# Two transformer blocks in split fp32 products: head, tables, expert hand-over and two stage entries rearranged

## The chip, the cores and the metric

The kernel runs on one core of one Trainium2 chip. The metric is the device time of one execution in microseconds (us), the median of several runs. The core has a matrix engine (TensorE, PE in the profile), two elementwise engines (VectorE, DVE; ScalarE, ACT), GpSimd (POOL), and SyncE (SP), which here only requests transfers. PEclk is the share of TensorE's full clock that was granted.

## The reference

256 tokens of width 1024 go through two blocks, all in fp32. Cut to its core:

```python
def first_block(x, ...):
    x = x + short_conv_mixer(rmsnorm(x, norm_mix[0]), w_in, w_conv, w_out)   # c_gate * u, 3-tap conv, b_gate
    x = x + swiglu(rmsnorm(x, norm_ffn[0]), w_gate, w_up, w_down)            # width 2816
    x = x + mla_mixer(rmsnorm(x, norm_mix[1]), ...)                          # 8 heads, latent q and kv
    return x + moe_swiglu(rmsnorm(x, norm_ffn[1]), router, ...)              # 8 experts of 2048, top 2

def second_block(x, ...):
    proj = rmsnorm(x, attn_norm_g) @ w_in                 # qa, ka, va, qb, kb, vb
    out_a = gqa_axial_attention(rope(norm(qa)), rope(norm(ka)), va)
    out_b = rmsnorm(differential_attention(norm(qb), norm(kb), vb, lam, rel_bias), b_subln_g)
    x = x + concatenate([out_a, out_b]) @ w_out
    return x + square(relu(rmsnorm(x, mlp_norm_g) @ w_up)) @ w_down          # width 4096
```

## The kernel before

Every product is made of three. A weight is split in two parts: `w_hi` is a rounding copy made by ScalarE (L115), `w_lo` what is left, made by VectorE (L116), and the activations are split likewise; hi times hi, lo times hi and hi times lo are added in PSUM (`mm3`, L231). PSUM has 8 banks of 128x512.

Weights come in loads of 1 MB, requested by SyncE (`load`, L96) into a ring of seven slots (`raws`); while the experts run, three more slots (`raws2`, L845) belong to the ring. A load is split into two units of 128x1024 (`split`, L107), for which a ring of five pairs exists (`units`). `weight_parts` (L159) is a generator that gives the units in the order in which the stages use them. `get` (L210) takes the next and keeps one more made; `prepare(n)` (L216) makes n of them at once, so that their splits stand earlier on ScalarE and VectorE. Each engine does its instructions in program order as the scheduler leaves it. `behind(...)` (L85) orders what is issued inside it after the given instructions, and `fence` holds instructions which the next split must follow.

The stages: the head (`first_norm`, L358) squares x, scales it by the rms factor and the gain, transposes it into `hT` (features on partitions) and splits it. The short convolution has twelve loads of `w_in`, each for two products of `proj_T` (L236), in the order c, u, b. At the end of each stage an `Entry` (L400) adds the sums to x, multiplies by the next gain (`xg`), transposes and splits, one half of the tokens (t) at a time; the rms factor follows later. The second half's entry (`finish`) stands inside the next stage's first products. Inside the dense layer small tables (rope frequencies, gains, bias rows, lambda vectors, router weights) are requested behind the second gated pair (L644 to L647), by ScalarE's queue.

The experts run one after the other over at most 128 gathered tokens. `gather` (L1017) picks the tokens of two experts by products with a one-hot `pick`; `wide` (L1040) makes gate and up, `turned_features` transposes, the down product collects in `yb`. `gated_y` (L1049) multiplies by the gate and splits into `y`; `scatter` (L1057) puts the rows of one expert back by products with the one-hot `put`, and adds to x.

In the second block `columns_in` (L1160) makes 256 columns of the joint input projection for both halves; the first are the keys (`keys_a`), whose result is rotated and normed into `yd` and transposed (L1205), then the queries (`yq`). The MLP's first two products are made for one half of the tokens, then for the other.

## Time and profile before

| what | us |
|---|---|
| median of 3 runs (1299.24 to 1303.44) | 1300.73 |
| the profiled execution's own time | 1304.09 |
| its span | 1302.3 |
| TensorE busy in it | 1267.9 |
| VectorE, ScalarE busy | 994.9, 801.7 |

The rows further below come from this one execution. A timeline row has the start, the duration, the engine, the line in the kernel, the operation, `out<-in`, the shape and a count where like instructions follow one another; in brackets stands how long the engine was idle before it and what ended that. "Q" behind an engine's name is its queue of requests.

### The profile page before, as it was taken

What the parts mean: (1) busy time and instruction counts of PE and PEld (TensorE: products, weight loads), DVE (VectorE), ACT (ScalarE), POOL (GpSimd) and SP (SyncE); (2) the same over time, 40 slices, a digit from 0 to 9 for tenths busy, and PEclk for the clock granted to TensorE, in tenths of its full rate; (3) what the DMA queues carried; (4) which work ended last, traced back from release to release, by engine and by line L of the source; (5) the groups of instructions that cost most, each with busy time, mean ns of one, the idle gap of its engine ahead of it and who ended that gap; (6) DMA issues with size and microseconds to landing.
All of it is one profiled execution on the core that took longest, in us unless ns stands there. A gap on an engine that the chain in (4) does not pass through costs nothing.

```text
span 1302.3 us, 17506 instructions
## 1 busy us (share of the span) xinstructions
PE 1267.9 (97%) x6551; PEld 1065.9 (82%) x6551; DVE 994.9 (76%) x1283; ACT 801.7 (62%) x1089; POOL 76.3 (6%) x96
## 2 busy tenths in 40 slices
PE   8999999999998999999999999999998999999998
PEld 7998788888777888888888887878787887888887
DVE  6665655556867999999988989898898697765654
ACT  5444445445665877778867776777766566544442
POOL 0000100000502000000000000000000432000000
PEclk9999999999998999999999999999998999999999
DMA  9854655744434999989999999989987533456620
GB/s 318 280 168 175 217 192 129 245 142 149 163 127 174 372 379 353 374 306 360 356 335 320 326 359 337 349 324 361 349 307 243 177 106 114 144 188 196 192 97 33
DMA packets 156799, 320.26 MB, mean 246 GB/s; under 512 B 7788, under 2 KB 50823, under 8 KB 156712
## 3 DMA queue, kind: packets, MB, share of 16 engines
q1 hardware_dynamic: 151104, 313.54, 68.5%
q10 hardware_dynamic: 5608, 5.58, 1.8%
q8 instruction: 52, 0.85, 0.3%
q14 instruction: 35, 0.29, 0.1%
HBM read 317.00 MB, written 2.10 MB: 245 GB/s over the span
## 4 chain that ended last, share of the span: by engine, by line
PE 62%; DVE 2%; ACT 1%; POOL 1%; DMA 1%; issue 1%; POOLq 0%; ACTq 0%
PE bank L58 38%; PE yb L58 13%; PE acc L58 8%; PE bank L1076 1%; DVE w_lo L116 1%; PE po L58 1%; ACT w_hi L115 1%; DMA bias<-wide_d 1%; POOL yq L1198 0%; DMA raw<-in_moe_w_up_dram 0%; PE bank L1279 0%; POOL s L1301 0%; ACT s L1295 0%; POOL raq L1185 0%; PE bank L392 0%
## 5 line engine op out<-in xcount | busy, mean ns | idle before, releaser
L116 DVE TENSOR_TENSOR w_lo<-raw,w_hi 128x1024 fp32r<-128x1024 f32 (+2 forms) x600 | 709.6, 1218 | 189.6 <-ACT w_hi L115 177.4
L115 ACT CAST w_hi<-raw 128x1024 fp32r<-128x1024 f32 (+2 forms) x600 | 605.3, 1043 | 270.6 <-PE bank L58 149.1
L58 PE MATMUL bank<-w_hi,xT 128*128 128x512 f32 x1024 | 318.9, 393 | 0.9 <-ACT w_hi L115 0.9
L58 PEld LDWEIGHTS bank<-w_hi,xT 128*128 128x128 f32 x1024 | 190.4, 188 | 39.4 <-ACT w_hi L115 1.7
L58 PE MATMUL bank<-w_lo,xT 128*128 128x512 f32 x512 | 201.6, 394 | 1.1 <-DVE w_lo L116 1.1
L58 PE MATMUL bank<-w_hi,hT 128*128 128x256 f32 (+1 forms) x672 | 162.9, 338 | 2.4 <-ACT w_hi L115 2.0
L58 PEld LDWEIGHTS bank<-w_hi,hT 128*128 128x128 f32 x672 | 116.2, 192 | 15.8 <-ACT w_hi L115 2.3
L58 PE MATMUL bank<-hT,w_hi 128*128 128x256 f32 (+1 forms) x656 | 116.2, 326 | 2.2 <-DVE hT L394 1.4
L58 PEld LDWEIGHTS bank<-w_lo,xT 128*128 128x128 f32 x512 | 96.1, 188 | 26.2 <-DVE w_lo L116 6.4
L58 PE MATMUL bank<-w_lo,hT 128*128 128x256 f32 (+1 forms) x336 | 110.8, 337 | 0.0
L58 PEld LDWEIGHTS bank<-hT,w_hi 128*128 128x128 f32 x656 | 96.8, 194 | 11.1 <-DVE hT L394 1.7
L58 PE MATMUL yb<-w_hi,a_hi 128*128 128x512 f32 x256 | 101.3, 396 | 0.0
L58 PE MATMUL yb<-w_hi,a_lo 128*128 128x512 f32 x256 | 101.3, 396 | 0.0
L58 PE MATMUL yb<-w_lo,a_hi 128*128 128x512 f32 x256 | 95.6, 399 | 0.0
L58 PE MATMUL acc<-w_hi,a_hi 128*128 128x512 f32 x216 | 84.9, 393 | 0.0
L58 PE MATMUL acc<-w_lo,a_hi 128*128 128x512 f32 x216 | 84.4, 391 | 0.0
L58 PE MATMUL acc<-w_hi,a_lo 128*128 128x512 f32 x216 | 84.3, 390 | 0.0
L58 PEld LDWEIGHTS bank<-w_lo,hT 128*128 128x128 f32 x336 | 64.6, 192 | 6.9 <-DVE w_lo L116 0.5
L58 PE MATMUL bank<-hT,w_lo 128*128 128x256 f32 (+1 forms) x464 | 65.2, 284 | 0.0
L58 PEld LDWEIGHTS bank<-hT,w_lo 128*128 128x128 f32 x464 | 62.2, 194 | 2.3
L58 PEld LDWEIGHTS yb<-w_hi,a_lo 128*128 128x128 f32 x256 | 48.2, 188 | 11.3
L58 PEld LDWEIGHTS yb<-w_hi,a_hi 128*128 128x128 f32 x256 | 48.2, 188 | 11.4
(318 smaller groups left out, 1373.3 us busy)
## 6 DMA issues: line engine op xcount, KB each, us to landing
raw<-in_moe_w_gate_dram SPq DMA_DIRECT2D x64, 1024.0 KB, 6.5
raw<-in_moe_w_up_dram SPq DMA_DIRECT2D x64, 1024.0 KB, 6.6
raw<-in_moe_w_down_dram SPq DMA_DIRECT2D x64, 1024.0 KB, 6.4
raw<-in_w_up_dram SPq DMA_DIRECT2D x16, 1024.0 KB, 5.4
raw<-in_w_down_dram SPq DMA_DIRECT2D x16, 1024.0 KB, 4.9
raw<-in_conv_w_in_dram SPq DMA_DIRECT2D x12, 1024.0 KB, 12.1
raw<-in_ffn_w_gate_dram SPq DMA_DIRECT2D x11, 1024.0 KB, 5.1
raw<-in_ffn_w_up_dram SPq DMA_DIRECT2D x11, 1024.0 KB, 12.5
```

Source lines behind the costliest of these rows:

```text
L58: return nc.tensor.matmul(o, lhsT, rhs, start=start, stop=stop)
L115: halves[:] = [nc.scalar.copy(hv, v), nc.vector.tensor_tensor(lv, v, hv.bitcast(F32), op=OP.subtract)]
L116: nc.vector.tensor_tensor(lv, v, hv.bitcast(F32), op=OP.subtract)]
L1076: nc.tensor.transpose(bt[:, fs], sg[:, fs], ident)
```

## The change

**Head.** x is loaded in quarters and transposed as it is; the gain is multiplied behind the transposes, the rms factor only on the results (`inv_row`, a row made by one product of ones and a diagonal). The first 256 columns of `w_in` come in two loads of half size, and the first product runs in halves of the features. **Tables.** 21 requests go from ScalarE's queue to SyncE's. **Experts.** Copies of the gather all go to ScalarE; two experts' rows are put back in one sum; two units are prepared ahead of `gated_y`; the odd experts' `y` takes a slot of the three more. **Entries.** Ahead of the second block's attention and of its MLP, three and two units are prepared before the first products, and 512 columns of the first half of the tokens stand ahead of the second half's entry.

```diff
@@ -101,7 +102,7 @@
-        nc.sync.dma_start(v, src.rearrange("(a p) b -> p a b", p=P))
+        loads[:] = [nc.sync.dma_start(v, src.rearrange("(a p) b -> p a b", p=P))]
@@ -159,9 +160,14 @@
-        upper = [columns_of(w[:, g * D : (g + 1) * D]) for g in (1, 2, 0)]
-        for _ in range(0, KD, 2):
-            for u in upper:
+        for rs in blocks(2, 512):
+            v = load(w[rs, D : D + 256], 4, 256)
+            for fs in blocks(2):
+                yield split(v[:, :, fs])
+        upper = [columns_of(w[:, g * D : (g + 1) * D], 256 * (g == 1)) for g in (1, 2, 0)]
+        for f0 in range(0, KD, 2):
+            for u in upper[f0 == 0 :]:
                 yield next(u)
                 yield next(u)
@@ -213,6 +219,11 @@
+    def take(n):
+        prepare(n)
+        return [ready.pop(0) for _ in range(n)]
@@ -233,19 +244,30 @@
+    def first_proj_T(h):
+        banks = [bank()[:, :T] for _ in range(2)]
+        for n in range(2):
+            for o in banks:
+                hi, lo = get()
+                for w, s in ((hi, 0), (hi, 1), (lo, 0)):
+                    for k in range(4):
+                        mm(o, w[:, k], h[s][:, 4 * n + k], n == 0 and k == 0 and w is hi and s == 0,
+                           n == 1 and k == 3 and w is lo)
+        return banks
@@ -355,35 +377,67 @@
-    def first_norm(g):
+    def first_entry(g):
...
+        xg = acts.tile([P, 2, D], F32, tag="xn", name="xgT", bufs=1).rearrange("p a (b k t) -> p (a b) k t", b=2, k=4)
+        his, xgs, los = [], [], []
+        def multiplied(j):
+            t, n = quarters[j]
+            v = bank().rearrange("p (k t) -> p k t", k=4)
+            for k in range(4):
+                turned = nc.tensor.transpose(v[:, k], x[:, t, (4 * n + k) * P : (4 * n + k + 1) * P], ident)
+            xgs.append(nc.vector.tensor_tensor(xg[:, j], v, g[:, 4 * n : 4 * n + 4, None].to_broadcast([P, 4, P]),
+                                               op=OP.mult))
+            return turned
...
+        def rounded(j):
+            his.append(nc.scalar.copy(place(hi, j), xg[:, j]))
+        def left(j):
+            los.append(nc.vector.tensor_tensor(place(lo, j), xg[:, j], place(hi, j).bitcast(F32), op=OP.subtract))
...
+        for j in range(4):
+            with behind(*los[-1:], *xgs[-1:]):
+                turned = multiplied(j)
+            if j < 3:
+                with behind(*his[-1:]):
+                    rounded(j)
+            if j == 1:
+                with behind(xgs[1]):
+                    left(0)
+        with behind(xgs[3]):
+            left(1)
+        fence[:] = [his[2], los[1]]
+        prepare(2)
+        with behind(halves[0]):
+            rounded(3)
+        for j in (2, 3):
+            with behind(halves[1], los[-1]):
+                left(j)
+        fence[:] = [his[3], los[3]]
+        return (hi, lo), turned
...
+    def first_factors(pool):
+        ss, ms, inv, rs = (pool.tile([P, 2], F32, name=n, bufs=1) for n in ("ss0", "ms0", "inv0", "rs0"))
+        junk = acts.tile([P, D], BF16, tag="sg", name="junk")
+        with behind(*halves):
+            for t in range(2):
+                nc.scalar.activation(junk, x[:, t], AF.Square, accum_out=ss[:, t : t + 1])
+        nc.vector.tensor_scalar(ms, ss, 1.0 / D, EPS, op0=OP.mult, op1=OP.add)
+        nc.vector.reciprocal(inv, ms)
+        nc.gpsimd.tensor_tensor(rs, ms, mhalf[:, :2], op=OP.pow)
+        diag = pool.tile([P, 2, P], F32, name="diag", bufs=1)
...
+            nc.vector.tensor_scalar(diag[:, t], ident, inv[:, t : t + 1], None, op0=OP.mult)
+        return rs, diag
@@ -419,11 +475,17 @@
-            left = []
+            left, last = [], []
             for n, ns in enumerate(blocks(2, 512)):
-                if acc is not None:
+                stack = ExitStack()
+                stack.enter_context(behind(*last))
+                if acc is not None and self.factor is not None:
+                    nc.vector.scalar_tensor_tensor(x[:, t, ns], acc[n], self.factor[:, t : t + 1], x[:, t, ns],
+                                                   op0=OP.mult, op1=OP.add)
+                elif acc is not None:
                     nc.vector.tensor_tensor(x[:, t, ns], x[:, t, ns], acc[n], op=OP.add)
-                nc.vector.tensor_tensor(self.xg[:, t, ns], x[:, t, ns], g[:, ns], op=OP.mult)
+                stack.close()
+                last = [nc.vector.tensor_tensor(self.xg[:, t, ns], x[:, t, ns], g[:, ns], op=OP.mult)]
@@ -515,9 +577,9 @@
         rb = pool.tile([32, 4], F32, name="rb")
-        nc.scalar.dma_start(rb, i["rel_bias_2"])
+        nc.sync.dma_start(rb, i["rel_bias_2"])
         onehot = pool.tile([32, 512], F32, name="onehot")
-        nc.scalar.dma_start(onehot, i["c_bucket"])
+        nc.sync.dma_start(onehot, i["c_bucket"])
@@ -543,32 +605,43 @@
-        for b, ns in zip(g, blocks(2, 512)):
-            mm(b, one, row[:, ns], True, True)
-        turn_rows(rows, 0, 24)
+        ones = cp.tile([P, P], F32, name="ones_f", bufs=1)
+        nc.vector.memset(ones, 1.0)
+        turn_rows(g_rows, 32, KD)
+        h, turned = first_entry(cols[:, 32 : 32 + KD])
+        with behind(turned, fence[1]):
+            turn_rows(rows, 0, 24)
...
-            pc = proj_T(h, f0 == 0)
             c_sb = cp.tile([P, 2, T], F32, name="c_sb")
-            copied = nc.scalar.copy(c_sb, pc)
-            pu = proj_T(h)
+            if f0 == 0:
+                pc = first_proj_T(h)
+                first_rs, diag = first_factors(cp)
+                pu = proj_T(h)
+                b = bank()[:, :T]
+                with behind(products[-1]):
+                    mm(b, ones, diag.rearrange("p t k -> p (t k)"), True, True)
+                nc.scalar.copy(inv_row, b)
+                for f in range(2):
+                    nc.vector.tensor_tensor(c_sb[:, f], pc[f], inv_row, op=OP.mult)
+            else:
+                pc = proj_T(h)
+                nc.vector.tensor_tensor(c_sb, pc, inv_row[:, None, :].to_broadcast([P, 2, T]), op=OP.mult)
+                pu = proj_T(h)
...
-                with behind(copied):
+                with behind(done):
@@ -583,9 +656,10 @@
-        entry = Entry()
+        entry = Entry(first_rs)
@@ -629,7 +703,7 @@
                 prod = nc.vector.scalar_tensor_tensor(sg[t], pu[t], rs[:, t : t + 1], sg[t], op0=OP.mult, op1=OP.mult)
-            with behind(silu, prod):
+            with behind(silu, prod, *loads):
                 for table in tables if made[0] in (0, 2) else ():
                     next(table, None)
@@ -1015,18 +1089,18 @@
-            for src, dst, copy in ((h_hi, x_hi, nc.scalar.copy), (h_lo, x_lo, nc.vector.tensor_copy)):
+            for src, dst in ((h_hi, x_hi), (h_lo, x_lo)):
...
-                    copy(dst[:, k0 : k0 + 2], v)
+                    nc.scalar.copy(dst[:, k0 : k0 + 2], v)
...
-            put = ep.tile([P, T], F32R, name="put", bufs=2)
+            put = ep.tile([P, T], F32R, name="put", bufs=3)
@@ -1046,29 +1120,27 @@
-        def gated_y(place, yb, last):
-            y = room_y.tile([P, 2, D], F32R, tag="raw", name="y") if last else \
-                acts.tile([P, 2, D], F32R, tag="xn", name="y", bufs=1)
+        def gated_y(place, yb, odd):
+            y = (room_y if odd else acts).tile([P, 2, D], F32R, tag="raw" if odd else "xn", name="y",
+                                               **({} if odd else {"bufs": 1}))
...
-        def scatter(put, y, done=None):
...
+        def rows_back(rows, halves):
+            banks = [[bank() for _ in range(2)] for _ in halves]
+            for last, (put, y) in enumerate(rows):
+                for t, pair in zip(halves, banks):
+                    for s in range(2):
+                        for b, ns in zip(pair, blocks(2, 512)):
+                            mm(b, put[:, blocks(2)[t]], y[:, s, ns], last + s == 0, last + s == 2)
+            return banks
+        def scatter(rows):
+            for t in range(2):
+                for b, ns in zip(rows_back(rows, (t,))[0], blocks(2, 512)):
+                    nc.vector.tensor_tensor(x[:, t, ns], x[:, t, ns], b, op=OP.add)
@@ -1106,10 +1179,9 @@
-                if g == E * NC:
-                    prepare(3)
                 if c0 == NC - 1:
-                    done = gated_y(place, yb, g == E * NC)
+                    prepare(3 if g == E * NC else 2)
+                    rows.append(gated_y(place, yb, len(rows) == 1))
@@ -1122,12 +1194,8 @@
         entry = Entry()
-        def enter(t):
-            entry.half(t)
-            prepare(4)
-        scatter(*done, enter)
+        for t, banks in enumerate(rows_back(rows, (0, 1))):
+            entry.half(t, banks)
@@ -1157,13 +1225,33 @@
+        def first_columns_in():
+            os = [bank().rearrange("p (t c) -> p t c", t=2) for _ in range(2)]
+            ws = take(3)
+            part_in(os[0], ws, 0, range(KD))
+            ws = [ws[:2], ws[2:] + take(1)]
+            part_in(os[1], ws[1], 0, range(4))
+            rest_of_entry()
+            part_in(os[1], ws[1], 0, range(4, KD))
+            for o, w in zip(os, ws):
+                part_in(o, w, 1, range(KD))
+            return os
...
+            if first:
+                return first.pop(0)
...
-                if t and not bias:
-                    rest_of_entry()
@@ -1357,6 +1445,7 @@
+        first = first_columns_in()
@@ -1380,11 +1469,11 @@
-                ws = [get(), get()] if first and f0 == 0 else None
+                ws = take(2) if first and f0 == 0 else None
                 for ts in blocks(2) if ws else (slice(0, T),):
-                    if ts.start:
-                        entry.finish()
                     for f, o in enumerate(banks):
+                        if ws and f and ts.start == 0:
+                            entry.finish()
                         hi, lo = ws[f] if ws else get()
                         for k in range(KD):
```

TensorE at the program's start, before (`row` is the gain, `rows` the taps, `xn` the normed x):

```order
L58 MATMUL bank<-row,one 128x512 x2
L319 MATMUL bank<-ident,rows 128x24
L377 MATMUL bank<-ident,xn 128x128 x16
L58 MATMUL bank<-hT,w_hi 128x256 x8
L58 MATMUL bank<-hT,w_lo 128x256 x8
L58 MATMUL bank<-hT,w_hi 128x256 x24
L58 MATMUL bank<-hT,w_lo 128x256 x8
```

and after (`g_rows` is the gain as eight rows):

```order
L341 MATMUL bank<-ident,g_rows 128x8
L390 MATMUL bank<-ident,x 128x128 x16
L341 MATMUL bank<-ident,rows 128x24
L58 MATMUL bank<-hT,w_hi 128x256 x8
L58 MATMUL bank<-hT,w_lo 128x256 x4
L58 MATMUL bank<-hT,w_hi 128x256 x8
L58 MATMUL bank<-hT,w_lo 128x256 x4
L58 MATMUL bank<-hT,w_hi 128x256 x8
L58 MATMUL bank<-hT,w_lo 128x256 x4
L58 MATMUL bank<-hT,w_hi 128x256 x8
L58 MATMUL bank<-hT,w_lo 128x256 x4
```

The first product's six groups of eight became groups of eight and four by halves of the features, and the outer product of the gain is gone.

ScalarE between the second gate product and the next split in the dense layer, before (the last of its 21 table requests):

```order
L502 DMA axcs<-in_c_axial_dram 128x2x128
L69 DMA ga_q<-in_a_q_norm_g_dram 128x64
L69 DMA ga_k<-in_a_k_norm_g_dram 128x64
L69 DMA lam_q_1320<-in_lambda_q_2_dram 128x64
L69 DMA lam_k_1322<-in_lambda_k_2_dram 128x64
L69 DMA lam_q_1324<-in_lambda_q_2_dram 128x64
L69 DMA lam_k_1326<-in_lambda_k_2_dram 128x64
L546 DMA wr<-in_moe_router_dram 128x8x8
L115 CAST w_hi<-raw 128x1024 x2
```

and the start of the same requests on SyncE, after:

```order
L105 DMA raw<-in_ffn_w_up_dram 128x4x512 x2
L105 DMA raw<-in_ffn_w_down_dram 128x2x1024
L580 DMA rb<-in_rel_bias_dram 32x4
L582 DMA onehot<-in_c_bucket_dram 32x512
L355 DMA rows<-in_mla_q_norm_dram 1x128
L355 DMA rows<-in_mla_k_norm_dram 1x128
L355 DMA rows<-in_b_subln_g_dram 1x128
L352 DMA rows<-in_b_q_norm_g_dram 1x2x64
```

All but two of them (`low_gain`, four loads earlier) stand there. On ScalarE the split now follows the gate's `sg` directly; on SyncE the requests stand between two loads of `w_down`, and the loads behind them wait for the requests.

TensorE at the entry to the second block's attention, before (`y` and `put` are an expert's rows and their places, `xg` the entry's tokens, `w_hi` and `w_lo` the columns):

```order
L58 MATMUL yb<-w_lo,a_hi 128x512 x2
L58 MATMUL bank<-y,put 128x512 x4
L392 MATMUL bank<-ident,xg 128x128 x8
L58 MATMUL bank<-y,put 128x512 x4
L58 MATMUL bank<-w_hi,hT 128x256 x2
L58 MATMUL bank<-w_lo,hT 128x256
L58 MATMUL bank<-w_hi,hT 128x256 x2
L58 MATMUL bank<-w_lo,hT 128x256
```

after:

```order
L58 MATMUL bank<-y,put 128x512 x12
L446 MATMUL bank<-ident,xg 128x128 x8
L58 MATMUL bank<-w_hi,hT 128x256 x10
L58 MATMUL bank<-w_lo,hT 128x256 x8
L58 MATMUL bank<-w_hi,hT 128x256 x10
```

and then, from the second `xg` to the transposes of the keys (`yd`):

```order
L446 MATMUL bank<-ident,xg 128x128 x8
L58 MATMUL bank<-w_hi,hT 128x256 x4
L58 MATMUL bank<-w_lo,hT 128x256 x4
L58 MATMUL bank<-w_hi,hT 128x256 x12
L58 MATMUL bank<-w_lo,hT 128x256 x8
L58 MATMUL bank<-w_hi,hT 128x256 x16
L58 MATMUL bank<-w_lo,hT 128x256 x8
L58 MATMUL bank<-w_hi,hT 128x256 x8
L1293 MATMUL bank<-ident,yd 128x128 x4
```

All of the scatter now stands ahead of the first transposes, four of its sixteen products further ahead among the `yb` products. Between the second `xg` and `yd` stand 60 products, of which 24 follow the keys' columns; before it was 72, of which 48.

## Rows read from the trace of the kernel before

**Rows 1.** The page, part 1: busy time, share and instructions of each engine.
```profile
PE 1267.9 (97%) x6551; PEld 1065.9 (82%) x6551; DVE 994.9 (76%) x1283; ACT 801.7 (62%) x1089; POOL 76.3 (6%) x96
```

**Rows 2.** Timeline of the head: start, duration, engine, operation [idle before <-releaser].
```profile
2.46 3.75 PE L58 MATMUL bank<-row,one 1*128 1x512 f32 x4 [2.46 <-DMA row<-in_norm_mix_dram]
...
7.61 0.63 ACT L366 ACTIVATE xn<-x 128x512 f32<-128x512 f32 x1 [0.71 <-DMA x<-in_x_dram]
...
13.97 2.07 PE L58 MATMUL bank<-hT,w_hi 128*128 128x256 f32 x8 [0.77 <-ACT w_hi L115]
...
17.55 3.41 PE L58 MATMUL bank<-hT,w_hi 128*128 128x256 f32 x24
...
21.75 2.08 PE L58 MATMUL bank<-hT,w_hi 128*128 128x256 f32 x16
...
24.63 2.08 PE L58 MATMUL bank<-hT,w_hi 128*128 128x256 f32 x16
```

**Rows 3.** Transfer rate in 40 slots of 0.5 us from 0 to 20 us.
```profile
GB/s 0 0 0 29 160 336 380 288 156 188 274 340 313 313 360 381 375 381 367 352 352 348 350 342 352 352 342 354 346 344 350 348 350 348 344 352 346 348 348 346
```

**Rows 4.** Timeline of the dense layer around the small tables, 110 to 145 us.
```profile
116.71 1.99 PE L58 MATMUL bank<-w_lo,hT 128*128 128x512 f32 x8
...
118.53 2.43 PE L58 MATMUL bank<-w_hi,hT 128*128 128x512 f32 x10
...
120.70 0.33 ACTq L518 DMA_DIRECT2D rb<-in_rel_bias_dram  x1
...
131.50 0.75 DVE L630 SCALAR_TENSOR_TENSOR sg<-bank,rs,sg 128x512 f32<-128x512 f32 x1 [0.61 <-PE bank L58]
...
135.43 0.44 ACTq L546 DMA_DIRECT2D wr<-in_moe_router_dram  x1
...
135.92 1.99 ACT L115 CAST w_hi<-raw 128x1024 fp32r<-128x1024 f32 x2 [12.26 <-DMA ga_k<-in_a_k_norm_g_dram]
...
137.02 1.40 PE L58 MATMUL bank<-w_hi,hT 128*128 128x512 f32 x4 [2.03 <-ACT w_hi L115]
```

**Rows 5.** Stretch table: us, busy of PE, PEld, DVE, ACT, POOL, PEclk, DMA, GB/s.
```profile
136.00:142.00 6.00, 4.98 (x14) 3.69 (x15) 5.00 (x6) 6.00 (x8) 5.61 (x10) 0.72 0.33 81
```

**Rows 6.** Timeline of SyncE's own queue, 60 to 260 us.
```profile
124.00 14.62 SPq L104 DMA_DIRECT2D raw<-in_ffn_w_gate_dram  x2
```

**Rows 7.** The page, part 6: requests, KB each, us to landing.
```profile
raw<-in_ffn_w_up_dram SPq DMA_DIRECT2D x11, 1024.0 KB, 12.5
```

**Rows 8.** Timeline of TensorE behind an expert's rows, 768 to 796 us.
```profile
788.69 0.73 PE L58 MATMUL bank<-w_hi,xT 128*128 128x512 f32 x2 [0.43 <-ACT w_hi L115]
...
789.95 0.50 PE L58 MATMUL bank<-w_lo,xT 128*128 128x512 f32 x1 [0.53 <-DVE w_lo L116]
```

**Rows 9.** Stretch table of the experts, columns as in rows 5.
```profile
416.00:985.00 569.00, 567.00 (x2595) 463.70 (x2593) 517.24 (x512) 428.76 (x474) 0.00 (x0) 1.00 0.95 343
```

**Rows 10.** One tile's view: weight loads of the experts, 820 to 880 us.
```profile
DMA to landing us min/median/max: 7.4/7.8/8.5
```

**Rows 11.** Timeline of TensorE at the entry to the attention, 968 to 1032 us.
```profile
999.90 1.94 PE L392 MATMUL bank<-ident,xg 128*128 128x128 f32 x8 [2.71 <-DVE xg L426]
...
1001.49 2.06 PE L58 MATMUL bank<-y,put 128*128 128x512 f32 x4
...
1006.91 1.03 PE L392 MATMUL bank<-ident,xg 128*128 128x128 f32 x8
...
1017.49 0.63 PE L1205 MATMUL bank<-ident,yd 128*128 128x128 f32 x4 [0.54 <-PE bank L58]
...
1025.42 0.66 PE L1205 MATMUL bank<-ident,yq 128*128 128x128 f32 x4 [1.55 <-POOL yq L1198]
```

**Rows 12.** Timeline of VectorE in the same stretch.
```profile
996.73 1.23 DVE L116 TENSOR_TENSOR w_lo<-raw,w_hi 128x1024 fp32r<-128x1024 f32 x1
```

**Rows 13.** Timeline of TensorE at the entry to the MLP, 1103 to 1127 us.
```profile
1123.36 1.46 PE L58 MATMUL bank<-hT,w_hi 128*128 128x256 f32 x10 [1.41 <-DVE hT L394]
```

**Rows 14.** Timeline of VectorE in the same stretch.
```profile
1117.56 2.35 DVE L116 TENSOR_TENSOR w_lo<-raw,w_hi 128x1024 fp32r<-128x1024 f32 x2
```

More of the change, by code (lines that the diff above doesn't have):

```diff
@@ L63, in block_kernel @@
     x = const.tile([P, 2, D], F32, name="x")
-    for ns in blocks(2, 512):
-        nc.sync.dma_start(x[:, 0, ns], i["x"][0, :P, ns])
+    quarters = [(t, n) for n in range(2) for t in range(2)]
+    for t, n in quarters:
+        ns = blocks(2, 512)[n]
+        nc.sync.dma_start(x[:, t, ns], i["x"][0, t * P : (t + 1) * P, ns])
     def row_bcast(pool, src, n, name, queue=nc.scalar, **kw):
@@ L90, in behind @@
             yield
-    fence, halves = [], []
+    fence, halves, loads = [], [], []
     more, turn = [], [0]
@@ L124, in rows_of, with columns_of @@
                 yield split(v[:, k : k + 1])
-    def columns_of(w):
-        for c in range(0, w.shape[1], 256):
+    def columns_of(w, begin=0):
+        for c in range(begin, w.shape[1], 256):
             v = load(w[:, c : c + 256], KD, 256)
@@ L234, in mm3, with proj_T @@
         mm(o, a_hi, w_lo, False, stop)
-    def proj_T(h, fresh=False):
+    products = []
+    def proj_T(h):
         o = bank().rearrange("p (f t) -> p f t", f=2)
@@ L240, in proj_T @@
             hi, lo = get()
-            late, early = ((hi, h[1]), (lo, h[0])) if fresh and f == 0 else ((lo, h[0]), (hi, h[1]))
-            for k in range(KD):
-                mm(o[:, f], hi[:, k], h[0][:, k], k == 0, False)
-            for k in range(KD):
-                mm(o[:, f], early[0][:, k], early[1][:, k], False, False)
-            for k in range(KD):
-                mm(o[:, f], late[0][:, k], late[1][:, k], False, k == KD - 1)
-        return o
+            for w, s in ((hi, 0), (hi, 1), (lo, 0)):
+                for k in range(KD):
+                    products[:] = [mm(o[:, f], w[:, k], h[s][:, k], k == 0 and w is hi and s == 0,
+                                      k == KD - 1 and w is lo)]
+        return o
+    def first_proj_T(h):
[3 more added lines that the diff above has]
+                hi, lo = get()
+                for w, s in ((hi, 0), (hi, 1), (lo, 0)):
+                    for k in range(4):
+                        mm(o, w[:, k], h[s][:, 4 * n + k], n == 0 and k == 0 and w is hi and s == 0,
+                           n == 1 and k == 3 and w is lo)
+        return banks
     def proj(h, width, fresh=None, midway=None):
@@ new lines, in place @@
+        def place(z, j):
+            t, n = quarters[j]
+            return z[:, 4 * n : 4 * n + 4, blocks(2)[t]]
+        def rounded(j):
[11 more added lines that the diff above has]
+                    left(0)
@@ L397, in block_kernel, with __init__ @@
     class Entry:
-        def __init__(self):
+        def __init__(self, factor=None):
             self.both = hts.tile([P, KD, 2, T], F32R, tag="hT", name="hT")
@@ L407, in __init__ @@
             self.ss, self.ms, self.rs = (small.tile([P, 2], F32, name=n) for n in ("ss", "ms2", "rs2"))
+            self.factor = factor
         def half(self, t, acc=None):
@@ L1055, in gated_y @@
             return place[0], y
-        def scatter(put, y, done=None):
-            places = [(t, n) for t in range(2) for n in range(2)]
-            last = []
-            for t, n in sorted(places, key=lambda v: v if done else v[::-1]):
-                ts, ns = blocks(2)[t], blocks(2, 512)[n]
-                b = bank()
-                with behind(*last):
-                    mm(b, put[:, ts], y[:, 0, ns], True, False)
-                    product = mm(b, put[:, ts], y[:, 1, ns], False, True)
-                    add = nc.vector.tensor_tensor(x[:, t, ns], x[:, t, ns], b, op=OP.add)
-                if done:
-                    last = [product, add]
-                if done and n == 1:
-                    done(t)
+        def rows_back(rows, halves):
[10 more added lines that the diff above has]
+                    nc.vector.tensor_tensor(x[:, t, ns], x[:, t, ns], b, op=OP.add)
         def turned_features(sg):
@@ L1081, in block_kernel @@
         gather(pick)
-        a = yb = place = done = None
+        a = yb = place = None
+        rows = []
         for g in range(E * NC + 1):
@@ L1096, in block_kernel @@
                 nc.vector.scalar_tensor_tensor(sg, bu, slot_rs, sg, op0=OP.mult, op1=OP.mult)
-            if done is not None:
-                scatter(*done)
-                done = None
+            if len(rows) == 2:
+                scatter(rows)
+                rows = []
             if g:
@@ L1158, in rest_of_entry, with part_in @@
                             ap=[[2047, P], [512, 4], [1, T]]))
+        def part_in(o, ws, t, ks):
+            ts = blocks(2)[t]
+            for a, m in ((0, 0), (0, 1), (1, 0)):
+                for k in ks:
+                    mm(o[:, t], h[a][:, k, ts], ws[k // 4][m][:, k % 4], a + m + k == 0, a == 1 and k == KD - 1)
+        def first_columns_in():
[9 more added lines that the diff above has]
+            return os
         def columns_in():
+            if first:
+                return first.pop(0)
             o = bank().rearrange("p (t c) -> p t c", t=2)
```

61 lines of the change are left out of this document (16 added, 45 removed).

## The prediction

> **What bounds the kernel now.** I read the busy line first: TensorE is busy for 1267.9 of 1302.3 us [rows 1]. The change leaves TensorE the same products but for a handful in the head, so it can only win back the 34.4 us in which TensorE is idle, and time in which TensorE runs at half its clock. The profiled run took 1304.09 us, 1.8 more than its span, and 3.36 more than the median of the runs (1300.73). The sum below is made against 1304.09 and then moved down by 3.36. Next I read the timeline where TensorE waits, at the five places that the change touches: the head, the second gated pair of the dense layer, the experts, the entry to the second block's attention, and the entry to its MLP. The other idle time (latent attention, router, the heads of the second block, the last store) is not touched, and I leave it as it is.
>
> **Head.** Before, TensorE's first product of the first projection starts at 13.97 and the second projection at 21.75 [rows 2]. Two causes are seen there. The chain is long (squares, factor, scaled x, transposes, hi, lo), and the engine is slow: 16 products take 3.58 us at first (13.97 to 17.55), 0.22 each, where 24 take 2.88 later (21.75 to 24.63), 0.12 each. Of the 48 products the 32 behind 17.55 took 4.20, so they ran nearly all at the faster rate. So the clock rises from 1.2 to 2.4 GHz close behind 17.55; I put it 3.9 us after the first product. The changed head needs no factor before the transposes, and its first weights are half a load. What decides there is landing. Summing the slots of the transfer rate [rows 3], x (1.05 MB) has been moved by 6.0 us and half a load more (1.57 MB) by 7.5. From moved to usable took 1.6 for the last quarter of x (6.0, and its square at 7.61 [rows 2]); it cannot be under nothing. I keep 0.7 to 1.6, an estimate whose lower end halves the measured one. So the half load is there at 8.2 to 9.1, and its first hi part 0.6 later (the 128x512 pass at 7.61 took 0.63): the first product is at 8.8 to 9.7, and I take 9.45. With 3.9 us at 0.22 (17.5 products) and 30.5 at 0.12 (3.66) the 48 products end at 17.0 instead of 21.75: 4.75 won. Added is one fp32 product of 256 columns (sums turned to a row): 1024 such columns took 3.75 at half clock, so 0.47 at full. Multiplying by the factor on VectorE replaces a copy on ScalarE, beside products. Term: -4.3. Bounds: all 48 at 0.22 from 9.45 end at 20.0, with the added product at half clock (0.94) that is -0.8; all at 0.12 from 8.8 end at 14.5, that is -6.8.
>
> **Tables.** Before, ScalarE asks for 21 small tables from 120.70 to 135.43, and the next w_hi stands behind them: it starts at 135.92 after 12.26 us idle, and TensorE, which lived on the units of its ring, waits 2.03 for it at 137.02 [rows 4]. After that wait the clock is low: 0.72 granted over 6 us [rows 5], so 1.7 us are lost on top. If the requests leave ScalarE, w_hi goes on at its pace and both go: -3.75. SyncE gets the requests instead. They wait there for the second gate product (131.50 + 0.75), then take 21 x 0.44 = 9.2 us (one issue took 0.44 [rows 4]), and the weight loads stand behind them until about 142. What covers that are the loads in the ring: one load is 24 products of 512 columns (8 take 1.82, 116.71 to 118.53 [rows 4]), 5.4 us, and five of the seven slots in hand are 27 us, against 9.2 and the 12.5 us that the slowest kind of load in this stage took to land [rows 7]. Before, SyncE itself stood for 14.62 us between its issues at 124 without a shortage behind it [rows 6]. Bounds: -4.5 (VectorE's w_lo, also late there, comes early too) and 0 (a weight comes late in its place).
> The Trainium skill, "DMA: Bandwidth & Descriptors", section "Issuing engines are not separate DMA queues", says that starting transfers on several engines only saves the sequencer's time, usually small beside the transfer itself. By that rule the move would be worth next to nothing and the sum would be 3.75 higher. The trace disagrees as far as ScalarE's 12.26 idle us go: here the sequencer is the one that TensorE waits for. The same page, section "Queues, rings and completion order", gives SyncE and ScalarE one row of rings each, taken in ring order; by it the tables now stand in one line with the weights. That is the second rival below.
>
> **Experts.** Two stalls of 0.43 + 0.53 us, at 788.69 and 789.95 and again 147 us later, stand right behind the hand-over of an expert's rows, where ScalarE and VectorE make y before the next split [rows 8]. Now two units are prepared ahead of it: -1.9. The joined scatter has as many products; 16 additions to x fewer and 16 copies moved to ScalarE free VectorE, which is not the bound (517 busy of 569 us against TensorE's 567 [rows 9]): nothing. At the start four more copies stand on ScalarE ahead of the first units: +0.5 (bounds 0 and 2.5, four passes of 0.63). The rows of the odd experts now take a slot of the weight ring, so at three places a load is asked for only when the load two before it is split: +0.5 (see the last rival). Term -0.9, bounds -1.9 and +4.
>
> **Entry to the attention.** Before, the longest wait around the last scatter is 2.71 us and ends at 999.90, when x and x times gain are made behind one w_lo (1.23) [rows 11, 12]. That w_lo still stands there, so 999.90 stays for the second half of the transposes. But the four scatter products of the second half of the tokens (2.06 at 1001.49, at half clock) now lie in the idle time ahead of it. Since VectorE now makes x, gain, x, gain in turn, the second four transposes wait some 0.45 for theirs, so the columns start about 1.6 earlier. On the other side the transposes of the keys (1017.49) now have 24 products between them and the end of the keys' columns instead of 48: 2.88 less cover, of which I take +2.0. The wait for the queries (1.55 at 1025.42) then finds its work done: -1.55. Term -1.2, bounds -3.5 and +1.5.
>
> **Entry to the MLP.** TensorE waits 1.41 at 1123.36 [rows 13]; two w_lo (2.35) stand ahead of the x addition on VectorE [rows 14], and now one fewer: 1.18 earlier, of which I take -1.0. Bounds 0 and -1.4.
>
> **Sum.** -4.3 - 3.75 - 0.9 - 1.2 - 1.0 = -11.15: 1292.9 against the profiled 1304.09, and **1289.6** at the level of the median.
>
> **Rivals.**
> First, the head's clock stays low or the half loads land late: all 48 products at 0.22, -0.8 instead of -4.3: 1293.1. For it: the granted clock rose only after 3.9 us of products, and the changed head has a pause between its transposes and its products. Against: the transposes now run from about 4 us on. Chance 0.14.
> Second, the tables delay the weights: each table request on SyncE waits for older transfers, and a 1 MB load asked for behind them comes late. Then this place gives nothing: 1293.4. For it: 12.5 us to landing in this stage [rows 7]. Against: 27 us of cover. Chance 0.10.
> Third, the attention's chains pile up: the keys' transposes lose all 2.88 us, the clock falls in that gap as it did at 999.90 (8 transposes in 1.94 us, 8 in 1.03 at 1006.91 [rows 11]), and the queries' wait stays: +1.5 instead of -1.2: 1292.3. For it: ScalarE and VectorE make both halves' chains there at once. Chance 0.09.
> Fourth, on the other side: the odd experts' rows in the weight ring take away the lead of the loads. It has one place, the load behind y in experts 1, 3 and 5: it is asked for when the load two before it is split. One load lasts 569/192 = 2.96 us, so two are 5.9 us, against 7.8 to landing [rows 10] and a hi and a lo part (1.0 [rows 4] and 1.2 [rows 12], so 2.2): 4.1 short, and 1.7 at half clock behind it, three times: 17.4, so 1289.6 - 0.5 + 17.4 = 1306.5, slower than before. It decides once the splits stand less than three units (1.48 us each) ahead of TensorE; with the five units of their ring full they add 7.4 us of cover, and nothing is lost. For it: VectorE is 91% busy there, so the splits cannot catch up quickly. Against: TensorE waited under 2 us in 569 for them. Chance 0.06.
>
> **How the numbers follow.** The forecast has 0.61. Its own range, from the terms' bounds taken together as independent errors (about 2, 1.5, 2, 2 and 0.7, so 4) and the runs' own spread, is 1284.5 to 1295. The range for 8 in 10 takes in the first three rivals: 1283.5 to 1298. What a measurement can tell from no change is 0.3%, 3.9 us: 1296.8 to 1304.6 is the same. Faster: nearly all of the forecast and the first three rivals, 0.88. Same: their upper tails, 0.07. Slower: the fourth rival, 0.05.
>
> **What would show it.** In the changed profile the second projection starts near 17 (step one); no idle time over 2 us on ScalarE near 120 to 136, no half-clock stretch at 137, and SyncE's first weight behind the tables near 142 with nothing waiting for it (step two); no wait over 0.3 us behind an expert's y, and none at the three loads (step three); columns at about 1.6 us after the first transposes of the entry, a wait of about 2.5 us for the keys' transposes and none for the queries' (step four); a wait under 0.4 us in the MLP's entry (step five). The prediction is wrong if TensorE's idle time in the experts grows past 4 us, or if the head's clock stays at half beyond 14 us.

## The result and the profile after

The changed kernel takes 1292.81 us (median of 5 runs, 1291.45 to 1293.8) against 1300.73: ratio 0.9936, 95% interval 0.9922 to 0.9951, so 6.4 to 10.1 us faster, 7.9 in the medians. On the chip of the second set of experiments it was 0.9947 (0.9934 to 0.9961). The forecast of "faster" and its range held; the forecast gain, 11.15 us, was too large.

The two first profiles are further apart than the runs: the profiled execution of the changed kernel took 1291.77 us, 12.3 less than that of before. Its page, where [rows 1] stood before:

```profile
PE 1260.7 (98%) x6550; PEld 1064.6 (83%) x6550; DVE 979.9 (76%) x1258; ACT 809.8 (63%) x1101; POOL 74.1 (6%) x95
```

Head, TensorE (compare [rows 2]): the first product of the first projection starts at 10.58, the second projection at 18.02, and the added product takes 0.24 until the next starts.

```profile
10.58 2.07 PE L58 MATMUL bank<-hT,w_hi 128*128 128x256 f32 x8 [0.77 <-ACT w_hi L116]
...
13.31 1.52 PE L58 MATMUL bank<-hT,w_hi 128*128 128x256 f32 x8
...
18.02 2.08 PE L58 MATMUL bank<-hT,w_hi 128*128 128x256 f32 x16
...
23.79 0.60 PE L58 MATMUL bank<-diag,ones_f 128*128 128x256 f32 x2
24.03 1.18 PE L58 MATMUL bank<-hT,w_hi 128*128 128x256 f32 x7
```

Tables, SyncE's queue (before [rows 4, 6]): 19 of the 21 are requested from 109.06 to 121.04, a weight load right behind. TensorE waits for nothing there; the stretch table shows it busy for all of 132 to 138 at full clock, where [rows 5] had 0.72.

```profile
109.06 0.35 SPq L580 DMA_DIRECT2D rb<-in_rel_bias_dram  x1
...
120.61 0.43 SPq L608 DMA_DIRECT2D wr<-in_moe_router_dram  x1
121.17 0.51 SPq L105 DMA_DIRECT2D raw<-in_ffn_w_down_dram  x1
```
```profile
132.00:138.00 6.00, 6.00 (x32) 5.04 (x32) 3.32 (x5) 3.07 (x4) 0.00 (x0) 1.00 1.05 389
```

Experts, TensorE: of the four stalls of [rows 8] one of 0.32 us is left, and one of 0.53 is new. SyncE's queue shows the hold that y in the ring brings: nothing is requested from 559.36 to 576.36, when the last product that puts rows back has just ended (576.32), and the third time ScalarE waits for a load at 856.57.

```profile
782.44 0.50 PE L58 MATMUL bank<-w_lo,xT 128*128 128x512 f32 x1 [0.32 <-DVE w_lo L117]
858.94 0.51 PE L58 MATMUL bank<-w_lo,xT 128*128 128x512 f32 x1 [0.53 <-DVE w_lo L117]
```
```profile
559.36 0.37 SPq L105 DMA_DIRECT2D raw<-in_moe_w_down_dram  x1
576.36 0.37 SPq L105 DMA_DIRECT2D raw<-in_moe_w_up_dram  x1
```
```profile
572.43 3.89 PE L58 MATMUL bank<-y,put 128*128 128x512 f32 x16
```
```profile
856.57 2.95 ACT L116 CAST w_hi<-raw 128x1024 fp32r<-128x1024 f32 x3 [1.89 <-DMA raw<-in_moe_w_up_dram]
```

Entry to the attention, TensorE and VectorE (compare [rows 11, 12]): the first four transposes wait 2.34 us, the second four 1.24, the keys' 2.03, the queries' none. The same w_lo (1.22) stands ahead of x. The columns start 2.35 behind the first transposes; before, it was 3.45 (999.90 to 1003.35, the last line). Behind the keys' wait the granted clock is low.

```profile
988.21 0.66 PE L446 MATMUL bank<-ident,xg 128*128 128x128 f32 x4 [2.34 <-DVE xg L488]
990.10 0.81 PE L446 MATMUL bank<-ident,xg 128*128 128x128 f32 x4 [1.24 <-DVE xg L488]
990.56 2.48 PE L58 MATMUL bank<-w_hi,hT 128*128 128x256 f32 x10
...
1006.64 0.63 PE L1293 MATMUL bank<-ident,yd 128*128 128x128 f32 x4 [2.03 <-issue]
...
1014.35 0.60 PE L1293 MATMUL bank<-ident,yq 128*128 128x128 f32 x4
```
```profile
985.13 1.22 DVE L117 TENSOR_TENSOR w_lo<-raw,w_hi 128x1024 fp32r<-128x1024 f32 x1
...
988.07 0.68 DVE L486 TENSOR_TENSOR x<-x,bank 128x512 f32<-128x512 f32 x1
988.67 1.29 DVE L488 TENSOR_TENSOR xg<-x,gain 128x512 f32<-128x512 f32 x2
```
```profile
1007.00:1011.00 4.00, 4.00 (x24) 4.00 (x22) 4.00 (x11) 0.71 (x2) 3.19 (x2) 0.57 0.60 246
```
```profile
1003.35 0.63 PE L58 MATMUL bank<-w_hi,hT 128*128 128x256 f32 x2
```

Entry to the MLP: a wait of 0.74 us for the transposes, where [rows 13] had 1.41 behind them.

```profile
1109.03 0.66 PE L446 MATMUL bank<-ident,xg 128*128 128x128 f32 x4 [0.74 <-DVE xg L488]
```

Cut at the same instructions (the marks), the two kernels' executions (each profiled twice) compare as follows. At the mark of the last down product the changed kernel has four more scatter products (0.9 us) still to do than the one before; around `gate,pick` two products stand in another order, so the two rows next to that mark are read as a sum. The last row sums, up to the last instruction, what the granted clock falls short of full: 1 us at half clock (0.5 granted, 1.2 GHz) counts 0.5. This is what "lost" means below, and it is the most that half clock can cost, since it costs nothing while TensorE waits. (Summed on past the last instruction, the four are 11.6, 6.5, 9.2 and 13.1; the 9.2 in an expectation below is such a sum.)

| us from the mark before to | before | before, again | changed | changed, again |
|---|---|---|---|---|
| dense layer, second entry (its wait of 0.24) | 114.75 | 114.55 | 111.26 | 111.56 |
| latent attention, first wait (0.27) | 205.04 | 202.90 | 200.91 | 200.92 |
| router, second half (0.24) | 83.84 | 83.83 | 83.85 | 83.84 |
| first expert's `gate,pick` | 13.44 | 12.23 | 12.97 | 12.84 |
| last down product | 577.46 | 577.50 | 573.93 | 573.89 |
| first transposes of scores | 46.18 | 45.53 | 46.66 | 47.34 |
| last b keys | 42.42 | 42.42 | 42.41 | 43.76 |
| last product | 214.68 | 214.69 | 213.74 | 213.71 |
| lost at half clock | 10.5 | 5.4 | 8.5 | 12.0 |

The stretches agree to 0.1 us between two executions of a kernel, but for the start, for the wait behind the tables (2.03 and 1.32), and for places where the clock was at half in one and not in the other. That is what makes two executions of one kernel differ by 2 to 4 us.

### The profile page after: what moved, and what is told of

It is laid out like the page before. It is cut to its first block, busy times and chain, and to the rows that moved or that the text cites. A ratio compares the mean times of both kernels' runs of the same rounds, so it can differ in the third digit from the quotient of the medians.

```text
span 1290.2 us, 17528 instructions
## 1 busy us (share of the span) xinstructions
PE 1260.7 (98%) x6550; PEld 1064.6 (83%) x6550; DVE 979.9 (76%) x1258; ACT 809.8 (63%) x1101; POOL 74.1 (6%) x95
## 4 chain that ended last, share of the span: by engine, by line
PE 63%; DVE 3%; ACT 1%; issue 1%; POOL 1%; DMA 0%; ACTq 0%; DVEq 0%
PE bank L58 40%; PE yb L58 13%; PE acc L58 8%; DVE w_lo L117 1%; PE bank L1148 1%; PE po L58 1%; DMA raw<-in_moe_w_up_dram 0%; ACT w_hi L116 0%; PE bank L1367 0%; POOL s L1389 0%; ACT s L1383 0%; DVE x L486 0%; PE bank L446 0%; DVE xg L488 0%; DVE mx L1379 0%
## 5 line engine op out<-in xcount | busy, mean ns | idle before, releaser
L58 PE MATMUL bank<-w_lo,hT 128*128 128x256 f32 (+1 forms) x336 | 106.5, 337 | 0.0
```

The costliest lines, as they stand in the source:

```text
L58: return nc.tensor.matmul(o, lhsT, rhs, start=start, stop=stop)
```

## The experiments

**Before, once more** (nothing edited).

> The kernel before, unchanged, profiled once more. Theory A (the profiled execution of before was like all others): the wait for w_hi behind the table requests is again about 2 us with about 1.7 us of half clock behind it, ScalarE idle about 12 us there, and the span is near 1302. Theory B (that wait depends on how fast the small transfers land and was long by chance in that execution): the wait behind the requests is under 1 us, no half clock near 137, and the span is near 1298.5.

1299.98 us, span 1298.1. TensorE's wait behind the tables was 1.32 us, and the clock stayed full behind it:

```profile
136.06 1.19 PE L58 MATMUL bank<-w_hi,hT 128*128 128x512 f32 x4 [1.32 <-ACT w_hi L115]
```
```profile
135.00:141.00 6.00, 4.87 (x20) 3.73 (x21) 4.96 (x6) 6.00 (x8) 5.62 (x10) 1.00 0.35 77
```

Neither theory quite: ScalarE's queue is as slow as before (11.55 us idle), the wait is 0.7 shorter, and the half clock behind it came in one execution and not in the other. It followed in two of the six executions with the tables on ScalarE (behind 2.03 and 1.44), and not behind 1.27, 1.32, 1.34 and 1.44.

**Tables on SyncE alone.**

```diff
-        nc.scalar.dma_start(rb, i["rel_bias_2"])
+        nc.sync.dma_start(rb, i["rel_bias_2"])
...
-            with behind(silu, prod):
+            with behind(silu, prod, *loads):
```

> The kernel before with only the table requests moved to SyncE. Theory A: 4.1 us faster, as the two profiles show between the two places (1296.6, ratio 0.9968). Theory B: at most 1 us faster (1299.7 or more), since in most executions of before the wait is short.

1299.89 us, ratio 1.0002 (0.9991 to 1.0012): nothing that could be measured. Yet the wait is gone and the stretch is 201.00 instead of 202.90. The granted clock of the timed runs, known for each, says where the gain can have gone: 0.991 to 0.993 in all 12 (median 0.992), where the 27 of before have 0.991 to 0.996 (median 0.995). As (1 - clock) x span, an estimate from the rounded clocks, that is 10.4 us lost against 6.5: up to 3.9 us more half clock, enough to take back the 1.9. The one trace shows part of it: its router lost 5.1 us, as in the first profile of before, where that of "before, again" lost 3.4:

```profile
399.00:410.00 11.00, 7.57 (x40) 7.20 (x40) 7.91 (x20) 7.46 (x14) 4.51 (x4) 0.53 0.83 303
```
```profile
403.00:411.00 8.00, 4.31 (x26) 4.00 (x25) 6.58 (x18) 5.77 (x11) 3.48 (x2) 0.57 0.89 323
```

**The head alone** (`first_entry`, `first_factors`, `first_proj_T` and half loads in the kernel before).

> The kernel before with only the new head. Both theories: 3.5 us faster (1297.2, ratio 0.9973), the second projection starting near 18.0 instead of 21.75. If the head's gain is taken back later (weights that come later behind the half loads), under 1.5 us.

1297.19 us, ratio 0.9984 (0.9974 to 0.9994): 2.1 us. The stretch to the dense layer's entry is 111.02 against 114.75 and 114.55; the interval holds the 3.5 only at its end. Nothing is given back later in its trace (202.90, 83.88, 577.49 as before). But the start differs between executions of one kernel: with the old head the same entry comes at 112.43 to 114.75 in four traces, with the new one at 110.46 to 111.56 in ten, and the means are 2.6 apart.

**The changed kernel with the tables on ScalarE.**

> The changed kernel with the table requests back on ScalarE. Theory A: 4.1 us slower than the changed kernel, 1297 (ratio to before 0.997). Theory B: at most 1 us slower, 1293 to 1294. In its profile ScalarE is idle for about 12 us around the requests under both; they differ in how long TensorE waits behind them.

1292.91 us, ratio 0.9953 (0.9939 to 0.9967). The stretch is 202.83 again, with a wait of 1.27 us at 133.02. So the tables cost 1.9 us in an execution without half clock there; the intervals of the times overlap. The clocks differ as they did between the kernel before and "tables alone": median 0.995 in these ten runs (0.989 to 0.995), 0.991 to 0.993 in all ten of the changed kernel.

**The changed kernel, once more.**

> The changed kernel, unchanged, on the same chip as the ones below. Between the entry of the dense layer's wait and the latent attention's first wait 200.9 us, in the experts (gate,pick to the last down product) 573.9, as in its first profile. Theory C (what differs between executions of one kernel is where TensorE's clock is at half): the router stretch is 5.7 or 6.9 us by chance and the sum of half-clock time differs from the first profile (9.2 us lost). Theory D (the clock's course belongs to the program): 6.92 again and 9.2 lost again. Time 7 to 8 us under before.

1291.49 us. The stretches without half clock came out as before (200.92, 573.89), and the half clock elsewhere: 3.4 instead of 1.7 us lost at the entry, and 1.7 among the heads, where the first execution lost none behind the same waits. That is theory C, though the keys' 1.7 and the router's 5.1 came both times:

```profile
1042.00:1047.00 5.00, 4.10 (x22) 4.10 (x23) 4.94 (x11) 2.38 (x9) 0.85 (x1) 0.66 0.52 180
```

**No units prepared ahead of y.**

```diff
-                    prepare(3 if g == E * NC else 2)
+                    if g == E * NC:
+                        prepare(3)
```

> The changed kernel without the two units prepared ahead of the experts' y (the last expert's three stay). If the preparing took away the stalls behind y: waits of 0.43 and 0.53 us are back behind at least two experts' y, and the experts take 2 to 3 us longer (576 to 577). If it was the relief of VectorE (copies and additions gone): under 0.5 us difference.

1298.23 us, ratio 0.9991: nearly the whole gain of the change is gone, and more than either theory had. The experts take 580.98. The stalls are back behind three experts' y, and at 864.02 there is one of 2.49 us with half clock behind it: that is where SyncE had stood (no request from 834.97 to 857.57), and the load came too late.

```profile
708.33 0.74 PE L58 MATMUL bank<-w_hi,xT 128*128 128x512 f32 x2 [0.37 <-ACT w_hi L116]
709.59 0.49 PE L58 MATMUL bank<-w_lo,xT 128*128 128x512 f32 x1 [0.52 <-DVE w_lo L117]
...
864.02 0.73 PE L58 MATMUL bank<-w_hi,xT 128*128 128x512 f32 x2 [2.49 <-ACT w_hi L116]
```

**Odd experts' y in a slot of its own, ring of nine.**

```diff
-MORE_BUFS = 3
+MORE_BUFS = 2
...
+            y = (room_y if odd else acts).tile([P, 2, D], F32R, tag="yo" if odd else "xn", name="y", bufs=1)
```

> The changed kernel with the odd experts' y in a slot of its own, and two instead of three more slots for the weights (a ring of nine). If y in the ring is what holds the loads: SyncE no longer stands 17 us before a load of experts 2, 4 and 6, the wait of 0.53 us at 859 and that of 0.32 at 782 are gone, and the experts are 0.8 to 1.2 us shorter (573). If a shorter ring costs as much: the experts take 574 or more.

1291.62 us against 1291.49: no difference. The stall of 0.53 is gone, one of 0.32 stands at 781.66 and one at 927.48, and the experts take 574.07. With two units prepared, the hold costs nothing that a shorter ring doesn't cost too.

**Old order of the first columns.**

```diff
-        first = first_columns_in()
+        first = []
...
+                if t and not bias:
+                    rest_of_entry()
```

> The changed kernel with the old order of the first columns of the second block's projection (one group of 256 columns, the second half's entry between its two halves); the scatter stays joined and ahead. If the columns ahead are what the entry gains by: 1 to 2 us slower from the last down product to the first scores (47.5 now). If they only move the wait from the queries to the keys: within 0.5 us, with a wait of about 0.5 for the keys' transposes and 1.5 for the queries'.

1293.56 us, ratio 0.9960 (0.9946 to 0.9973), 2.1 us slower in the medians with overlapping intervals. The wait moves to the queries as the second theory says, but it is longer than the one it replaces, and the stretch to the scores is 47.89 instead of 46.66. So the columns ahead give about 1.2 us, and what they give up is seen in the keys' 2.03.

```profile
1004.71 0.63 PE L1295 MATMUL bank<-ident,yd 128*128 128x128 f32 x4 [0.36 <-PE bank L58]
...
1013.77 0.66 PE L1295 MATMUL bank<-ident,yq 128*128 128x128 f32 x4 [2.67 <-POOL yq L1288]
```

**The kernel before with two units prepared ahead of y.**

```diff
                 if c0 == NC - 1:
+                    if g < E * NC:
+                        prepare(2)
                     done = gated_y(place, yb, g == E * NC)
```

> The kernel before with one addition: two units prepared ahead of each expert's y. If the preparing alone is the gain of the experts: the four waits of 0.43 and 0.53 us are gone and the experts take 574.5 to 575 us instead of 577.5 (each pair costs 1.4 us of TensorE's steps, not the 0.96 that the trace calls idle); some 2 to 3 us faster than before. If the joined scatter and the moved copies were needed for it: under 1 us.

1297.49 us, ratio 0.9983 (0.9974 to 0.9992): 2.4 us. The experts take 575.12 instead of 577.46 and 577.50; two stalls of 0.32 remain. That one addition is most of what the experts win by the change.

**Transposes a step later, and with the third unit behind the first columns** (the first kernel has the first two pieces of the edit, the second all of them).

```diff
             yield
+            yield
             turn(akT, yd.rearrange("p t j c d -> p t j (c d)"), nc.scalar.copy)
...
-            tasks += at.get(step, [])
+            new = at.get(step, [])
+            tasks = tasks[:1] + new[:1] + tasks[1:] + new[1:] if step == 3 else tasks + new
...
-                    prepare(3 if g == E * NC else 2)
+                    prepare(2)
...
-            ws = take(3)
-            part_in(os[0], ws, 0, range(KD))
-            ws = [ws[:2], ws[2:] + take(1)]
+            ws = [take(2)]
+            part_in(os[0], ws[0], 0, range(KD))
+            ws.append(take(2))
```

> The changed kernel with the transposes of the keys one step later, and those of the first queries behind the next columns. If the wait of 2.03 us for the keys is only a matter of what stands ahead of it: it is gone, with the half-clock stretch behind it, and the stretch from the last down product to the last b keys is 2 to 3.5 us shorter (1289). If it comes back in front of the first scores (which need both transposes): a wait of 1 to 2 us there and under 1 us won.

> As the one before, and the third unit of the columns is split only behind the first 256 columns, so that no w_lo stands ahead of the entry's x on VectorE. If that w_lo (1.22 us) is what the transposes of the entry wait for: their wait falls from 2.34 to about 1.1 and the kernel is another 1 to 1.3 us faster (1287.5 to 1288). If the wait then moves to the third unit: no difference to the one before.

1286.81 us, ratio 0.9894 (0.9879 to 0.9909), and 1285.67, ratio 0.9889 (0.9874 to 0.9904): both beat both kernels; between the two the intervals overlap. With the transposes later, 2.03 becomes a wait of 1.04 before the scores, and the other waits between them shrink too: from the first transposes of the entry to the last b keys it takes 79.6 us instead of 83.8. With the third unit later the first wait is 1.28 instead of 2.34, and no half clock is left from 984 to 1020:

```profile
987.21 0.66 PE L446 MATMUL bank<-ident,xg 128*128 128x128 f32 x4 [1.28 <-DVE xg L488]
...
1015.99 1.14 PE L58 MATMUL bank<-akT,aqT 64*128 64x256 f32 x8 [1.04 <-ACT sq L1263]
```
```profile
984.00:1020.00 36.00, 32.23 (x258) 30.50 (x257) 31.19 (x61) 19.95 (x29) 12.08 (x8) 1.00 0.69 232
```

**The fastest with the tables on ScalarE.**

> The fastest version (transposes a step later, third unit later) with the table requests back on ScalarE. If the move is worth the 2.0 us that the dense layer's stretch is shorter by: about 1287.7, ratio 0.9905 to before against 0.9889, and a stretch of 202.8 instead of 200.9. If it is given back at the router, as the runs of before with the tables alone suggest: within 0.7 us (ratio 0.989 to 0.9895), with a router stretch of 12.2 or 12.3 us where the moved tables had 12.9.

1286.87 us, ratio 0.9904 (0.9888 to 0.9921) against 0.9889. Its profiled execution had the half clock behind the tables (204.60 us). The intervals overlap: that the tables' move gains in the timed runs is likely from the stretches and not shown by the times. Here the move brings no more half clock with it: 0.995 to 0.996 with the tables on SyncE, 0.995 to 0.997 on ScalarE, and the two ratios are 0.0015 apart, 2 us.

## Why the prediction was right, and which terms were off

- **In all.** Taken one by one, the terms came out at about 1.9 (tables, 3.75 forecast), 2.6 (head, 4.3), 3.1 (experts, 0.9), 0.4 (attention, 1.2) and 1.0 (MLP, 1.0). That the sum stayed near is luck in part: the experts gave 2.2 more than was forecast, and three other terms some 4.3 less.
- **Level.** The sum was moved down by 3.36, as if every stall of the profiled execution were in the median run as well. That execution had lost 10.5 us at half clock, the next one 5.4. What was subtracted as a level was in part what the tables term counted. This is why the profiles differ by 12.1 us in span, close to the 11.15 forecast, and the runs by 7.9. The runs' clocks show a loss that no term had: 0.994 to 0.996 in 59 of the 64 timed runs of the kernel before whose clock is known, 0.991 to 0.993 in all ten of the changed one. As (1 - clock) x span that is 6.5 us in the median against 9.0 and 10.3 in the two sets of five, so up to 2.5 to 3.8 us of the gain went back to half clock.
- **Tables, -3.75.** The wait is always there, the 1.7 us of half clock only in two of six. Without it the stretch is 1.9 to 2.0 shorter. The step on SyncE was also wrong in its course: the requests did not wait for the second gate product, they were made from 109.06 on, took 12.0 us instead of 9.2, and the cover was never tried. The second rival did not come: no weight was late. The Trainium skill's sentence in "DMA: Bandwidth & Descriptors", section "Issuing engines are not separate DMA queues", that the issuing engine saves little, fits the times (1.0002) better than the term did; the 1.9 us of the stretches say that it is not nothing, and the clocks of the runs that something was given back. Tables and weights in one queue did no harm that a run here shows.
- **Head, -4.3.** 3.0 to 3.7 in the stretches of the first traces, 2.1 timed alone, 2.6 between the means of all 14. The first product came at 10.58 and 10.08, where 9.45 was taken (9.48 to 10.58 in ten traces): ScalarE's first w_hi is ordered behind the third quarter's hi part and starts at 9.91, so not landing alone sets it.
- **Head, the clock.** This is the step that failed. The slow rate (0.21 to 0.22 us a product) was taken to last 3.9 us behind the first product, 17.5 products. In the first changed profile that held (17 products, 12 of them in 2.73 us, and from 14.66 on four in 0.48), but by luck: in the ten traces with the new head it is 15 to 28 products, 3.4 to 6.1 us, and the fast rate begins at 13.3 to 15.9, in nine of them past the 14 us that the prediction named as a sign of being wrong. With the old head it is 0.2 to 4.4 us; in the run "two units prepared ahead" the products are fast almost from the first (the lines below), and the second projection starts at 19.44 instead of 21.75. So the first product comes 3.8 earlier in the means (9.95 instead of 13.73), the second projection 2.9, and the added product takes 0.24. The profile's granted clock is 1.00 in all of the head; the rate is read from the products alone. The first rival (all 48 at half clock) did not come.

```profile
13.29 1.22 PE L58 MATMUL bank<-hT,w_hi 128*128 128x256 f32 x8 [1.08 <-ACT w_hi L115]
...
19.44 2.08 PE L58 MATMUL bank<-hT,w_hi 128*128 128x256 f32 x16
```

- **Experts, -0.9.** The mis-sized term: 3.1 us between the first profiles, whose routers both lost 5.1 (590.9 to 586.9, less the 0.9 still to do). The stalls were counted as the idle time shown (1.9), while preparing two units alone brought 2.4; the costs set against it did not come (from the first `pick` product to the first lo product it takes 6.95 to 7.76 us in the changed kernels, 6.98 to 7.68 in those before).
- **Fourth rival.** SyncE does stand, but not for the two loads' time (5.9) that was reckoned: 17.0, 15.6 and 18.5 us, and the first two times the next request follows when TensorE has put y's rows back, a condition that the prediction didn't have. Its price is not there: 0.53 us at one place, and nothing against a ring without the hold. It would have become real without the units prepared ahead (2.49 us at 864.02).
- **Attention, -1.2.** 0.4 came between the first profiles, which both lost 3.4 at half clock there; between the second ones (1.7 and 5.1 lost) the stretch grew by 0.9. The keys' wait and the queries' vanished wait were as forecast (2.03, none). The columns started 1.1 us earlier, not 1.6, because VectorE made another x and two more xg (988.07 to 989.96) before the second four transposes, which so waited 1.24, not 0.45. And one part of the third rival did come: behind the keys' 2.03 the clock fell, in all five traces that have this wait, and 1.7 us were lost that the term didn't have.
- **MLP, -1.0.** 0.94 to 0.98: right in size. A wait of 0.74 is left, where under 0.4 was expected.

Open: what in the tables' move brings the half clock. The router lost 5.1 us in seven of the eight traces with the tables on SyncE and in three of the six with them on ScalarE, but that makes the stretch only 1.2 us longer (13.44 and 12.23 in the table), each trace is one execution, and what decides the clock there was not found.

## What to carry to other kernels

Profile the kernel before twice and cut both at the same instructions before a term is sized: what repeats to 0.1 us is the program, and most of what does not was the clock here. Then compare the granted clocks of the timed runs as well: a change can win a wait and lose it again to half clock. A stall's price is the step from the instruction ahead to the one behind: at each hand-over of an expert's rows the idle time shown was 0.43 + 0.53, and the steps there were 1.5 us longer than without the stalls. When products are moved ahead of a wait, count what is left between each chain's start and its use.

## What the runs showed of the hardware

At the router 3.4 or 5.1 us were lost in all 14 traces, behind waits of 1.53 and 1.90 us; behind the keys' wait of 2.03 it was 1.7 in all five traces that have it. Elsewhere 1.7 or 3.4 were lost, or none: the same wait of 1.44 us behind the tables was followed by half clock in one kernel's execution and by none in another's, and the same waits among the heads (0.63 and 1.32) in two of the 11 executions that have them. In the head the products went from 0.21 to 0.12 us each between 0.2 and 6.1 us behind the first one, with a granted clock of 1.00 throughout. Of two programs with the same products, one had a granted clock of 0.991 to 0.993 in all of 12 runs, the other 0.994 to 0.996 in 25 of 27.
